# Two layers of a hybrid decoder trunk on one core: attention scores in two visits of one head each, another PSUM pool for the last transposes, and an opening in program order

## The chip, the cores and the metric

The kernel runs on one core of a Trainium2 chip. It computes two whole decoder layers in one launch. The metric is the device time of one execution in microseconds (us), lower is better; a time is the median of several runs. A profiled execution gives a trace with the start and the duration of each instruction on TensorE (PE, with its weight loads as PEld), VectorE (DVE), ScalarE (ACT), GpSimd (POOL) and the DMA queues.

## The reference

Input is `x` (256 tokens of 1024 values), a memory `mem` (256 x 1024), positions, and the weights of both layers, all fp32. Each layer does this:

```python
proj = x @ w_in[l]                                  # 1024 x 7680
q, k, v, cb, cc, cu, qm, gates = jnp.split(proj, IN_SPLITS, axis=-1)
q = rope(q, cos, sin); k = rope(k, cos, sin)        # 8 heads, each with two halves of 64
# differential attention, causal, per head: two softmaxes, one output
sc = einsum('bhcqd,bhckd->bhcqk', qb, kb) * scale   # c = 0, 1
p = softmax(where(causal, sc, -inf)); a = p[:, :, 0] - lam * p[:, :, 1]
o = a @ v; o = o * rsqrt(mean(o * o) + RMS_EPS) * subln_g * (1 - lam_init)
y_conv = short_gated_conv(cb, cc, cu, conv_w[l])    # 3 taps
y_mem = memory_attention(qm, mem, w_mem_kv[l])      # 4 heads over 256 memory tokens
g = sigmoid(gates)
merged = g0 * (y_attn @ w_br_attn) + g1 * (y_conv @ w_br_conv) + g2 * (y_mem @ w_br_mem)
x = layer_norm(ALPHA * x + merged @ w_out, ...)
x = layer_norm(ALPHA * x + grouped_moe(x), ...)     # 16 experts, top 2 of one group of 4
```

## The kernel before, in words

**Stages.** Per layer: keys and values of the memory (`mem_units`, `mv_units`), the transposed input `xT` (`transposed`), the projections with the attention woven between them (`mixers`, `proj`, `attention`, `mem_attention`), the gates, branches and output projection (end of `mixers`), then the router and the experts (`moe`). Weights stream in through SyncE's queue in tiles `raw` of 1 MB, several tiles ahead of their use.

**Split matmuls.** Outside the experts every weight tile is split into a high and a low part, in two halves: ScalarE writes the high part (`hl<-raw`, L180), VectorE the low part (`hl<-raw,hl`, L182). A block of a projection (`ws_block`, L218 to L221) is then 24 matmuls of 256 columns; a unit of `mv_units` (L354) is 12 matmuls of 512. Each such block or unit is one step of a generator and counts as 2600 in the weaving.

**Order of the work.** TensorE's instructions stand in the order in which the program writes them. VectorE's, ScalarE's and GpSimd's are placed by a scheduler, which orders them by its own reckoning; once built, each engine goes through its list strictly in that order.

**The weaving.** In `mixers`, four pairs of attention heads (p = 0 to 3) and two pairs of memory heads (p = 4, 5) are jobs; each job is a generator that is visited with `next(job)`, and `fill(n)` issues blocks of the projections worth n in between. Before the first visit of pair p, blocks are issued until the keys of the pair are in the program; that point comes with the issue of one block of the next projection. A pair of attention heads goes like this: the scores of both heads (`k,q`, L521); on VectorE the causal mask (L526), the maxima (L528) and their scale (L530); on ScalarE the exponentials (L535); on VectorE the reciprocal (L538) and the difference of the two softmaxes (L539 to L543); then TensorE transposes the probabilities (L551), ScalarE copies them (`aT`, L553), TensorE multiplies with the values (L561 to L563), and the result is normalised (`sq` L568, `ss` on GpSimd, `on` L574). The last step, four transposes of `on` (L579) and a split (L209, L210), is made in the middle of the next pair's job.

Before, the visits and fills of a pair are: scores of both heads, fill 5200, last step of the previous pair, fill 5200, transposes of the probabilities, fill 2600, values.

**Keys and queries.** Each projected q or k tile is turned by the rotary tables: four copies on ScalarE (`sw`, L462 and L463), two multiplications and an addition on VectorE (L465 to L467). The tables `sin` and `cos` are made once, in the opening: some 30 small instructions on VectorE (L373 to L392) and two activations on ScalarE (L395, L397).

**PSUM.** `bank()` takes one of four banks of the group "g" (projections, transposes) or one of four of the group "acc" (attention, accumulators). A head's scores take two "acc" banks, the transposed probabilities of a head one, the values of a pair one.

**The opening.** `prow` holds small parameters as rows; TensorE turns them into columns (L408), VectorE derives sums from them (`columns`, L410 to L425), TensorE adds these over partitions (`sums`, L434 and L441), and ScalarE and VectorE read the sums (L435 to L445).

## Time and profile before

| | before |
|---|---|
| median of 3 runs | 1175.45 us (1171.26 to 1175.72) |
| profiled execution, its own time | 1174.08 us |
| its span, first to last instruction | 1172.3 us |
| TensorE busy | 1073.3 us, 92% of the span |
| VectorE busy | 527.9 us, 45% |
| ScalarE busy | 419.4 us, 36% |
| granted TensorE clock, mean | 0.967 of full speed |

How to read it: the span leaves 1.8 us of the profiled execution's time outside. TensorE is busy nearly all the time, so time is lost where it idles or where its clock is granted at half speed (1.2 instead of 2.4 GHz).

### The profile page before, as it was taken

To read this page: it belongs to the slowest core of one execution; us is meant where nothing else is said; L and a number is where in the kernel's file an instruction comes from. 1 tells how busy PE (TensorE), PEld (TensorE's weight loads), DVE (VectorE), ACT (ScalarE), POOL (GpSimd) and SP (SyncE) were. 2 spreads that over 40 slices of the span, in tenths; PEclk is the share of its full clock that TensorE was granted. 3 is DMA by queue.
4 is the path that set the end of the run, shared out by engine and by line. 5 is a ranking of instruction groups with operands and counts; after the bars stand their busy time and mean duration, and the time that the engine had idled before them with its cause. 6 is when DMAs were issued, how large, how long until landed. Compare 5 with 4: busy or idle time off the path is not lost. (4 is left out here: it accounts for less than half of the span.)

```text
span 1172.3 us, 16735 instructions
## 1 busy us (share of the span) xinstructions
PE 1073.3 (92%) x6917; PEld 790.2 (67%) x6917; DVE 527.9 (45%) x874; ACT 419.4 (36%) x730; POOL 42.0 (4%) x87
## 2 busy tenths in 40 slices
PE   4998899999996999999979989999999789999995
PEld 4887899999985334343468868999999543344332
DVE  6667657555544111111367687565546511111114
ACT  3657644444432111010147576454444311011111
POOL 2000000000002000000010000000000110000001
PEclk8999899999998999999989989999999989999998
DMA  9933424556594999999999334345657769999993
GB/s 314 327 121 109 132 84 128 163 185 188 192 369 150 420 421 421 421 422 420 410 303 305 108 101 125 100 144 182 189 194 257 297 262 421 422 421 421 420 420 150
DMA packets 118609, 311.76 MB, mean 266 GB/s; under 512 B 5426, under 2 KB 83440, under 8 KB 93952
## 3 DMA queue, kind: packets, MB, share of 16 engines
q1 hardware_dynamic: 116192, 304.63, 70.2%
q0 software_dynamic: 1760, 5.35, 1.2%
q8 instruction: 56, 0.92, 0.3%
q10 hardware_dynamic: 576, 0.66, 0.2%
q14 instruction: 25, 0.20, 0.0%
HBM read 309.57 MB, written 1.05 MB: 265 GB/s over the span
## 5 line engine op out<-in xcount | busy, mean ns | idle before, releaser
L182 DVE TENSOR_TENSOR hl<-raw,hl 128x1024 fp32r<-128x1024 f32 x192 | 231.2, 1223 | 119.5 <-ACT hl L180 119.2
L218 PE MATMUL ps_g<-th,hl 128*128 128x256 f32 x960 | 244.5, 291 | 20.5 <-ACT hl L180 20.5
L180 ACT ACTIVATE hl<-raw 128x1024 fp32r<-128x1024 f32 x192 | 198.2, 1060 | 127.2 <-PE ps_g L221 60.0
L219 PE MATMUL ps_g<-tl,hl 128*128 128x256 f32 x960 | 240.3, 287 | 0.0
L971 PE MATMUL ps_g<-raw,xg 128*64 128x512 f32 x1024 | 229.4, 598 | 0.0
L218 PEld LDWEIGHTS ps_g<-th,hl 128*128 128x128 f32 x960 | 188.1, 196 | 24.3 <-ACT hl L180 22.0
L219 PEld LDWEIGHTS ps_g<-tl,hl 128*128 128x128 f32 x960 | 188.3, 196 | 0.3
L971 PEld LDWEIGHTS ps_g<-raw,xg 128*64 128x64 f32 x1024 | 71.7, 137 | 134.2 <-issue 131.5
L221 PE MATMUL ps_g<-th,hl 128*128 128x256 f32 x960 | 136.4, 285 | 0.5 <-DVE hl L182 0.5
L221 PEld LDWEIGHTS ps_g<-th,hl 128*128 128x128 f32 x960 | 125.4, 194 | 0.8 <-DVE hl L182 0.8
L1006 PE MATMUL ps_g<-raw,hT 128*64 128x512 f32 x512 | 113.6, 595 | 0.0
L208 DVE TENSOR_TENSOR yl<-ps_g,yh 128x512 fp32r<-128x512 f32 x32 | 22.1, 690 | 150.0 <-ACT yh L207 150.0
L1006 PEld LDWEIGHTS ps_g<-raw,hT 128*64 128x64 f32 x512 | 36.3, 137 | 67.6 <-issue 65.2
L207 ACT ACTIVATE yh<-ps_g 128x512 fp32r<-128x512 f32 x32 | 19.2, 598 | 117.1 <-PE ps_g L1006 117.1
L984 DVE SCALAR_TENSOR_TENSOR h<-ps_g,gs,gate 128x512 f32<-128x512 f32 x16 | 17.8, 1112 | 89.4 <-PE ps_g L971 89.4
L354 PE MATMUL ps_g<-hl,th 128*128 128x512 f32 x192 | 54.4, 417 | 2.0 <-ACT lexp L435 1.5
L995 ACT ACTIVATE hT<-ps_g 128x256 f32<-128x256 f32 x16 | 6.2, 385 | 116.9 <-PE ps_g L993 116.9
L354 PEld LDWEIGHTS ps_g<-hl,th 128*128 128x128 f32 x192 | 37.5, 202 | 12.8 <-issue 2.0
L915 PE MATMUL ps_g<-pf,xh 128*128 128x256 f32 x128 | 30.1, 321 | 13.4 <-DVE pf L898 13.4
L915 PEld LDWEIGHTS ps_g<-pf,xh 128*128 128x128 f32 x128 | 22.9, 218 | 25.5 <-issue 25.1
L920 ACT ACTIVATE xg<-ps_g 128x512 f32<-128x512 f32 x16 | 9.6, 598 | 77.6 <-PE ps_g L915 77.6
L996 DVE COPY hT<-ps_g 128x256 f32<-128x256 f32 x16 | 6.8, 424 | 67.6 <-ACT hT L995 67.6
(235 smaller groups left out, 1302.1 us busy)
## 6 DMA issues: line engine op xcount, KB each, us to landing
raw<-in_w_in SPq DMA_DIRECT2D x64, 1024.0 KB, 5.7
raw<-in_w_exp_gate SPq DMA_DIRECT2D x64, 1024.0 KB, 12.6
raw<-in_w_exp_up SPq DMA_DIRECT2D x64, 1024.0 KB, 14.2
raw<-in_w_exp_down SPq DMA_DIRECT2D x64, 1024.0 KB, 17.0
raw<-in_w_mem_kv SPq DMA_DIRECT2D x8, 1024.0 KB, 12.5
raw<-in_w_br_attn SPq DMA_DIRECT2D x8, 1024.0 KB, 5.1
raw<-in_w_out SPq DMA_DIRECT2D x8, 1024.0 KB, 5.0
raw<-in_w_br_conv SPq DMA_DIRECT2D x8, 512.0 KB, 3.6
```

Source lines behind the costliest of these rows:

```text
L180: nc.scalar.activation(hi, src, AF.Copy)
L182: nc.vector.tensor_tensor(lo, src, hi.bitcast(F32), op=OP.subtract)
L207: return (nc.scalar.activation(hi, src, AF.Copy), nc.vector.tensor_tensor(lo, src, hi.bitcast(F32), op=OP.subtract))
L208: nc.vector.tensor_tensor(lo, src, hi.bitcast(F32), op=OP.subtract))
L218: mm(dst, wh[:, k0 + k, :], ah[:, k, :], start=(k == 0), stop=False)
L219: mm(dst, wh[:, k0 + k, :], al[:, k, :], start=False, stop=False)
L221: mm(dst, wl[:, k0 + k, :], ah[:, k, :], start=False, stop=(k == n - 1))
L354: mm(b[t], a[:, k, t * 128:(t + 1) * 128], ww[:, kk, :], start=(k == 0 and a is ah and ww is wh), stop=(k == KD - 1 and ww is wl))
L915: mm(b[:, a], xs[:, t, (k + a) * 128:(k + a + 1) * 128], pf[:, t], start=(i == 0 and t == 0), stop=(i == 1 and t == 1))
L971: mm(b[both[i]], xg[:, k, c + i * CAP:c + (i + 1) * CAP], w[i][:, kk, :], start=(k == 0), stop=(k == KD - 1))
L984: nc.vector.scalar_tensor_tensor(h.rearrange("q f p -> q p f"), u.rearrange("q (p f) -> q p f", f=4), GS[p // 2][:, p % 2:p % 2 + 1], g.re ...
L1006: mm(bs[c][both[i]], h[:, 2 * j + f, both[i]], w[i][:, f, c * 512:(c + 1) * 512], start=(j == 0 and f == 0), stop=(j == 1 and f == 1))
```

## The change

The scores of a pair are issued in two visits, one head each: `yield` moves into the loop over the heads, in `attention` and in `mem_attention`. The fills of a pair become: fill 2600 (not for the first pair), scores of the first head, fill 2600, last step of the previous pair, scores of the second head, fill 5200, transposes of the probabilities, fill 2600, values. The last transposes of a pair take a bank of the group "g" instead of "acc". And the opening, from the first transposes to the rotary tables, is put under a manual order for VectorE and ScalarE: the instructions written there keep their program order among themselves on these two engines; others may be placed between.

```diff
-APART = (5200, 5200, 2600)
+APART = (2600, 2600, 5200, 2600)
...
+    beginning = tc.manual_schedule(engines={mybir.EngineType.DVE, mybir.EngineType.Activation})
+    beginning.__enter__()
     mT = {0: transposed(mts.pop(0))}
...
         rope[name] = tab
+    beginning.__exit__(None, None, None)
...
             probs[h] = pr[0]
-        yield
+            yield
         aT = []
...
-        b = bank([128, 2, S], "acc")
+        b = bank([128, 2, S])
         for h in range(2):
             for qb in range(2):
                 nc.tensor.transpose(b[:, h, qb * 128:(qb + 1) * 128], on[:, h, qb, :], ident)
...
             probs.append(pr)
-        yield
+            yield
...
+            if prev:
+                fill(APART[0])
             next(job)
-            fill(APART[0])
+            fill(APART[1])
             if prev:
                 next(prev, None)
-            fill(APART[1])
             next(job)
             fill(APART[2])
+            next(job)
+            fill(APART[3])
             next(job)
             prev = job
```

Lines of the changed program from `beginning` on are two or three higher than before (L180, L182 and L207 to L221 stay; L462 is L465, L535 is L538, L553 is L556). The lists of GpSimd and SyncE are the same before and after, but for names and lines. TensorE's list has the same instructions, in the places that the fills say. ScalarE's has three table loads more.

**Place 1, ScalarE's list in the opening.** `sin`, `cos` are the rotary tables, `th` the high part of a transposed input, `hl` that of a weight half, `kv` a copy of finished memory keys (L339) or values (L359). Before:

```order
L397 ACT_TABLE_LOAD
L397 ACTIVATE sin<-r,cc 128x256
L395 ACTIVATE cos<-r 128x256
L207 ACTIVATE th<-ps_g 128x512 x4
L180 ACTIVATE hl<-raw 128x1024 x6
L339 ACTIVATE kv<-ps_g 128x512 x2
L207 ACTIVATE th<-ps_g 128x512 x2
L180 ACTIVATE hl<-raw 128x1024 x2
L207 ACTIVATE th<-ps_g 128x512 x2
```

Now:

```order
L207 ACT_TABLE_LOAD
L207 ACTIVATE th<-ps_g 128x512 x4
L180 ACTIVATE hl<-raw 128x1024 x2
L339 ACTIVATE kv<-ps_g 128x512
L180 ACTIVATE hl<-raw 128x1024 x2
L339 ACTIVATE kv<-ps_g 128x512
L180 ACTIVATE hl<-raw 128x1024 x2
L207 ACTIVATE th<-ps_g 128x512 x4
L180 ACTIVATE hl<-raw 128x1024 x7
```

The two tables went from the head of the list to a place after the first projections (`sin` ahead of the sums, `cos` behind them, each behind a table load of its own), the first six weight halves are cut into three twos with a key copy between them, and the exponentials that follow load their table again.

**Place 2, VectorE's list around the parameter columns** (`pcol` is the first copy of the columns, `wbs` the sums that the matmul L441 needs, `n` and `r` steps of the rotary tables). Before, the columns' instructions stand alone:

```order
L410 COPY pcol<-ps_g 128x62
L182 TENSOR_TENSOR hl<-raw,hl 128x1024
L412 TENSOR_TENSOR lpr<-pcol 128x2
L418 TENSOR_TENSOR wr_470<-wr_raw,pcol 128x128
L419 TENSOR_TENSOR wb<-wr_raw,pcol 128x128
L421 TENSOR_REDUCE wbs<-wr_470 128x16
L421 TENSOR_REDUCE wbs<-wb 128x16
L418 TENSOR_TENSOR wr_476<-wr_raw,pcol 128x128
L419 TENSOR_TENSOR wb<-wr_raw,pcol 128x128
L421 TENSOR_REDUCE wbs<-wr_476 128x16
L421 TENSOR_REDUCE wbs<-wb 128x16
L425 TENSOR_SCALAR subs<-pcol 128x1 x2
```

Now the last twelve of the 27 rows from `pcol` to the last `wbs` read:

```order
L385 SCALAR_TENSOR_TENSOR r<-n,ang 128x256
L422 TENSOR_TENSOR wb<-wr_raw,pcol 128x128
L386 SCALAR_TENSOR_TENSOR r<-n,r 128x256
L424 TENSOR_REDUCE wbs<-wr_473 128x16
L387 SCALAR_TENSOR_TENSOR r<-n,r 128x256
L424 TENSOR_REDUCE wbs<-wb 128x16
L389 TENSOR_SCALAR r<-r 128x256
L422 TENSOR_TENSOR wb<-wr_raw,pcol 128x128
L390 TENSOR_SCALAR n<-r 128x256
L424 TENSOR_REDUCE wbs<-wr_479 128x16
L391 TENSOR_TENSOR r<-r,n 128x256
L424 TENSOR_REDUCE wbs<-wb 128x16
```

The second rotary table is now made between the columns' instructions; fifteen rows of the same mixture stand ahead of these, and among all 27 are thirteen rotary steps, two weight halves and a multiplication with `sin`.

**Place 3, the second pair of heads in layer 0.** ScalarE before, after the eight exponentials of both heads (`yh` is the split of the first pair's last step, `aT` the copies of the transposed probabilities):

```order
L462 ACTIVATE sw<-ps_g 32x512
L463 ACTIVATE sw<-ps_g 32x512
L462 ACTIVATE sw<-ps_g 32x512
L463 ACTIVATE sw<-ps_g 32x512
L209 ACTIVATE yh<-ps_acc,subs 128x512
L180 ACTIVATE hl<-raw 128x1024 x2
L462 ACTIVATE sw<-ps_g 32x512
L463 ACTIVATE sw<-ps_g 32x512
L462 ACTIVATE sw<-ps_g 32x512
L463 ACTIVATE sw<-ps_g 32x512
L180 ACTIVATE hl<-raw 128x1024
L553 ACTIVATE aT<-ps_acc 128x384 x2
```

ScalarE now, after the four exponentials of the first head; the four exponentials here are those of the second head:

```order
L209 ACTIVATE yh<-ps_g,subs 128x512
L180 ACTIVATE hl<-raw 128x1024 x3
L465 ACTIVATE sw<-ps_g 32x512
L466 ACTIVATE sw<-ps_g 32x512
L465 ACTIVATE sw<-ps_g 32x512
L466 ACTIVATE sw<-ps_g 32x512
L180 ACTIVATE hl<-raw 128x1024 x2
L538 ACTIVATE p,sm<-ps_acc,sm 128x128
L538 ACTIVATE p,sm<-ps_acc,sm 128x256
L538 ACTIVATE p,sm<-ps_acc,sm 128x128
L538 ACTIVATE p,sm<-ps_acc,sm 128x256
L556 ACTIVATE aT<-ps_acc 128x384
```

The second head's exponentials went from a place ahead of all copies and weight halves to a place behind the rotary copies of the next pair's keys and five weight halves. VectorE's list at the same pair, from the second head's scaled maxima to its probabilities, before:

```order
L530 TENSOR_SCALAR sm<-sm 128x4
L539 TENSOR_SCALAR sm<-sm,nlam 128x2
L542 TENSOR_SCALAR p<-p,sm 128x128
L542 TENSOR_SCALAR p<-p,sm 128x256
L543 SCALAR_TENSOR_TENSOR p<-p,sm 128x128
L543 SCALAR_TENSOR_TENSOR p<-p,sm 128x256
L538 RECIPROCAL sm<-sm 128x4
L539 TENSOR_SCALAR sm<-sm,nlam 128x2
L542 TENSOR_SCALAR p<-p,sm 128x128
L542 TENSOR_SCALAR p<-p,sm 128x256
L543 SCALAR_TENSOR_TENSOR p<-p,sm 128x128
L543 SCALAR_TENSOR_TENSOR p<-p,sm 128x256
```

and now, from the scaled maxima (one row ahead of these) to the probabilities of the second head:

```order
L469 TENSOR_TENSOR sw<-sw,sin 128x512
L182 TENSOR_TENSOR hl<-raw,hl 128x1024
L468 TENSOR_TENSOR k<-ps_g,cos 128x512
L182 TENSOR_TENSOR hl<-raw,hl 128x1024
L541 RECIPROCAL sm<-sm 128x4
L470 TENSOR_TENSOR k<-k,sw 128x512
L542 TENSOR_SCALAR sm<-sm,nlam 128x2
L182 TENSOR_TENSOR hl<-raw,hl 128x1024
L545 TENSOR_SCALAR p<-p,sm 128x128
L545 TENSOR_SCALAR p<-p,sm 128x256
L546 SCALAR_TENSOR_TENSOR p<-p,sm 128x128
L546 SCALAR_TENSOR_TENSOR p<-p,sm 128x256
```

The rotary steps of the next keys and four weight halves now stand between the second head's maxima and its probabilities.

## Rows read from the trace of the kernel before

**Rows 1.** The page of the profile: the span and the busy time of each engine.

```profile
span 1172.3 us, 16735 instructions
...
PE 1073.3 (92%) x6917; PEld 790.2 (67%) x6917; DVE 527.9 (45%) x874; ACT 419.4 (36%) x730; POOL 42.0 (4%) x87
```

**Rows 2.** TensorE's waits, grouped: waiting group <- engine, tile and line that ended the wait: total us, count, the longest in us.

```profile
PE ps_acc L521 <- DVE k L467: 9.5, 5, 2.8
PE ps_acc L521 <- DVE on L574: 9.0, 2, 4.5
```

**Rows 3.** The timeline of TensorE: start us, duration us, engine, line, operation, tiles, count, and in brackets the idle time before it with what ended it. Scores of the second, third and fourth pair in layer 0, and of the first pair in layer 1.

```profile
95.22 1.58 PE L521 MATMUL ps_acc<-k,q 64*128 64x128 f32 x16 [1.66 <-DVE k L467]
...
119.90 1.64 PE L521 MATMUL ps_acc<-k,q 64*128 64x128 f32 x6 [4.48 <-DVE on L574]
...
148.54 2.42 PE L521 MATMUL ps_acc<-k,q 64*128 64x128 f32 x16 [2.76 <-DVE k L467]
...
642.45 1.36 PE L521 MATMUL ps_acc<-k,q 64*128 64x128 f32 x14 [0.68 <-DVE k L467]
```

**Rows 4.** Stretches after a wait in which the clock was low: start and end, length, busy time and count on each engine, the mean granted clock (PEclk), the DMA share, GB/s. Two stand at scores, the third in the opening, the fourth behind the matmul of the first exponentials.

```profile
119.90:125.22 5.32, 5.32 (x15) 3.90 (x16) 5.21 (x15) 1.73 (x8) 0.00 (x0) 0.50 0.20 71
148.54:152.53 3.99, 3.99 (x23) 3.31 (x24) 3.87 (x12) 0.62 (x3) 0.00 (x0) 0.57 0.38 107
20.11:26.23 6.12, 6.12 (x28) 6.12 (x29) 6.12 (x7) 4.67 (x5) 0.00 (x0) 0.50 1.08 360
62.67:67.19 4.52, 4.52 (x13) 3.56 (x14) 2.98 (x8) 2.93 (x6) 0.00 (x0) 0.62 0.55 182
```

**Rows 5.** Timeline of ScalarE at the second pair of layer 0.

```profile
98.44 0.37 ACT L535 ACTIVATE p<-ps_acc,sm 128x128 f32<-128x128 f32 x1 [5.32 <-DVE sm L530]
...
105.23 2.00 ACT L180 ACTIVATE hl<-raw 128x1024 fp32r<-128x1024 f32 x2
```

**Rows 6.** Timeline of VectorE at the second pair of layer 0.

```profile
96.18 0.76 DVE L526 TENSOR_TENSOR ps_acc<-ps_acc,cmask 128x256 f32<-128x256 f32 x2 [1.01 <-PE ps_acc L521]
...
100.20 0.18 DVE L538 RECIPROCAL sm<-sm 128x4 f32<-128x4 f32 x1 [0.41 <-ACT p L535]
...
101.14 0.74 DVE L543 SCALAR_TENSOR_TENSOR p<-p,sm 128x128 f32<-128x128 f32 x2
```

**Rows 7.** VectorE, grouped by line and form, from 94 to 180 us: line, tiles, shapes, count | busy us, mean ns | idle before.

```profile
L182 DVE TENSOR_TENSOR hl<-raw,hl 128x1024 fp32r<-128x1024 f32 x18 | 21.6, 1221 | 2.2 <-ACT hl L180 2.2
...
L467 DVE TENSOR_TENSOR k<-k,sw 128x512 f32<-128x512 f32 x3 | 2.1, 687 | 0.0
```

**Rows 8.** Timeline of TensorE at the second pair of layer 0.

```profile
98.75 1.12 PE L221 MATMUL ps_g<-th,hl 128*128 128x256 f32 x8
...
101.63 1.12 PE L221 MATMUL ps_g<-th,hl 128*128 128x256 f32 x8
...
106.33 1.19 PE L354 MATMUL ps_g<-hl,th 128*128 128x512 f32 x4 [0.27 <-ACT hl L180]
...
109.43 0.82 PE L551 MATMUL ps_acc<-ident,p 128*128 128x128 f32 x6
```

**Rows 9.** Timeline of TensorE in the opening.

```profile
8.50 3.46 PE L289 MATMUL ps_g<-ident,mt 128*128 128x128 f32 x15 [1.76 <-DMA mt<-in_mem]
20.11 0.58 PE L218 MATMUL ps_g<-th,hl 128*128 128x256 f32 x1 [8.14 <-ACT hl L180]
...
54.28 0.27 PE L408 MATMUL ps_g<-ident,prow 62*128 62x62 f32 x1
...
60.75 0.43 PE L441 MATMUL ps_g<-wbs,ones 128*128 128x64 f32 x2
62.67 1.20 PE L354 MATMUL ps_g<-hl,th 128*128 128x512 f32 x4 [1.48 <-ACT lexp L435]
```

**Rows 10.** Timeline of ScalarE in the opening.

```profile
8.75 1.28 ACT L397 ACT_TABLE_LOAD   x1 [8.75 <-DMA cc<-consts]
14.96 0.51 ACT L397 ACTIVATE sin<-r,cc 128x256 f32<-128x256 f32 x1 [4.93 <-DVE r L392]
...
17.06 2.04 ACT L207 ACTIVATE th<-ps_g 128x512 fp32r<-128x512 f32 x4
18.97 5.81 ACT L180 ACTIVATE hl<-raw 128x1024 fp32r<-128x1024 f32 x6
28.83 0.60 ACT L339 ACTIVATE kv<-ps_g 128x512 f32<-128x512 f32 x1 [4.05 <-PE ps_g L221]
...
60.54 0.59 ACT L462 ACTIVATE sw<-ps_g 32x512 f32<-32x512 f32 x1 [1.72 <-PE ps_g L221]
61.15 1.28 ACT L435 ACT_TABLE_LOAD   x1
62.45 0.24 ACT L435 ACTIVATE lexp<-ps_g 128x2 f32<-128x2 f32 x2
```

**Rows 11.** Timeline of VectorE in the opening.

```profile
6.94 0.29 DVE L373 CAST posf<-posi 128x256 f32<-128x256 int32 x1 [5.20 <-DMA posi<-in_positions]
...
16.41 0.29 DVE L392 TENSOR_SCALAR r<-r 128x256 f32<-128x256 f32 x1
...
54.59 0.22 DVE L410 COPY pcol<-ps_g 128x62 f32<-128x62 f32 x1 [0.35 <-PE ps_g L408]
...
57.61 0.38 DVE L421 TENSOR_REDUCE wbs<-wb 128x16 f32<-128x128 f32 x1
```

## The prediction

> **What bounds the kernel now.** I read the page first: TensorE is busy 1073.3 of 1172.3 us [rows 1], so only two things can pay: a wait of TensorE, or a stretch in which its clock is low. The grouped waits of TensorE come next. At the lines that the change touches they show two groups, both at the scores L521: 9.5 us for keys that are not turned yet and 9.0 us for `on` [rows 2]. The timeline places them [rows 3]: the second pair's scores start 1.66 late and the fourth's 2.76 late behind `k`, the third's 4.48 late behind `on`; both heads' scores take four "acc" banks, and the previous pair's values still hold one until `on` is made. Last the windows: behind the two longer waits the granted clock is at its lower level, 1.2 GHz, for 5.32 us (0.50) and mostly so for 3.99 us (0.57) [rows 4]. A stretch T at mean clock c loses (1 - c) x T: 2.66 and 1.72 us. Behind the wait of 1.66 no such stretch follows. Neither VectorE (45%) nor ScalarE bounds the kernel, but each is in order, and what stands in its list ahead of a head's softmax is late for TensorE.
>
> **What the change removes.** The one step (2600) ahead of the first head covers the two waits for `k`: a block of 24 matmuls takes 101.63 - 98.75 = 2.88 us [rows 8], more than 1.66 and 2.76. For `on`, the first head takes only two banks, and the second head comes two steps later than the scores stood before: 5.8 against 4.48. The first pair has no fill ahead, so its 0.68 in layer 1 stays [rows 3]. Waits: 9.5 + 9.0 - 0.7 = 17.8. Clock: 2 layers x (2.66 + 1.72) = 8.8. Together **26.6 us** less.
>
> **What it adds at the transposes of the probabilities (L551).** Before, four steps of 2600 lay between the last score and these transposes; that is why L551 came without a wait (at 109.43 no idle time is shown) [rows 8]. Now the second head has two. Two blocks are 5.8 us; at the second pair one block and one memory unit, 2.88 and 109.43 - 106.33 = 3.10, so 6.0 [rows 8]. The lone chain of a head, from the first mask at 96.18 to the end of its fused difference at 101.14 + 0.74 = 101.88, takes 5.7 [rows 6]. Cover and chain are equal, so all that stands between in the lists turns into a wait.
>
> At the **second pair** place 3 shows much between. The next keys' `sw` copies now come ahead of the second head's exponentials, and need the first block behind the scores: 2.88, and 0.3 for the hand-over (my choice; VectorE stood 0.41 before it took over from ScalarE at 100.20 [rows 6]). Then four copies of 0.59 [rows 10], 2.4; two weight halves, 2.0 [rows 5]; four exponentials, from 98.44 [rows 5] to the reciprocal behind them at 100.20 [rows 6], 1.7. Then VectorE: reciprocal to fused difference 100.20 to 101.88, 1.7 [rows 6], with the key addition 0.69 and one weight half 1.22 in between [rows 7], 3.6. Sum 2.88 + 0.3 + 2.4 + 2.0 + 1.7 + 3.6 = 12.9; less 6.0 gives a wait of 6.9 us. Bounds: 4.9 if the two weight halves run during the block, 8.1 if VectorE is one more half (1.22) behind.
>
> At the **other three pairs** less stands between. By the changed lists, the first pair has a table load, 1.28 [rows 10], and two low halves, partly within the first head's own time; the third has two low halves, 2 x 1.22 = 2.4 [rows 7], behind the first head's products, 1.7; the fourth has those products and a split of 0.7. I take 2.6 as the mean, with bounds 1 and 4. Waits: 2 x (6.9 + 3 x 2.6) = 29.4.
>
> Nothing here shows how the clock falls behind these waits. The nearest rows are the same engine's waits of 4.48 and 2.76 [rows 3, 4]. I take 2.66 for the second pair and 1.72 for two of the other three: 2 x 2.66 + 4 x 1.72 = 12.2; bounds 5.3 (only the second pair) and 16. Added at L551: **41.6 us**.
>
> **The last transposes' bank.** They move from an "acc" to a "g" bank. Taken at zero: no wait in the rows at these lines is for a "g" bank, and blocks run on both sides to cover a late one; without that cover it would be up to one copy, 0.6 [rows 10], for each of 8, so 0 to 4.8 in all. Memory heads get their two visits under the same fills; their chain has fewer steps, taken at zero too.
>
> **The opening.** Place 1: before, ScalarE made both tables first, and TensorE stood 8.14 us until 20.11 [rows 9]; the table steps ran on VectorE from 6.94 to 16.41 ahead of all else [rows 11]. Now the first transposes' copies lead. They end behind the last transpose, 8.50 + 3.46 = 11.96 [rows 9], plus one copy 0.6; then one weight half, 5.81 / 6 = 1.0 [rows 10]: the first block starts at about 13.7, 6.4 earlier. Taken back: the key copies (0.60 [rows 10]) now stand ahead of the third and fifth weight half, so the next block waits for a finished one plus copy plus half, 0.60 + 1.0 + some 0.3, twice: 3.8. Then place 2. L408 to L441 is 60.75 - 54.28 = 6.5 on TensorE [rows 9]. In that time VectorE had to do 58.0 - 54.59 = 3.4 with one weight half in it [rows 11]; now 27 rows: 2.2 without the half, 13 table steps of 0.3 = 3.9 (rows of 0.29), two halves 2.4, one multiplication 0.7: 9.2, and `pcol` itself starts up to 2 later because table steps stand ahead of it. 0.3 + 9.2 + 2 - 6.5 = 5.0 of wait at the second sums' matmul. The wait of 1.48 for the first exponentials [rows 9] goes inside it. Clock: the 6.12 us at 0.50 and 4.52 us at 0.62 [rows 4] move, not vanish: 0. Sum -6.4 + 3.8 + 5.0 - 1.5 = **about +1** (bounds -4 and +4).
>
> ScalarE's three added table loads are on the path in two places only, both counted: ahead of `sin`, and at the first pair. Each is the load's row, 1.28: a copy ends at 60.54 + 0.59 = 61.13, the load runs from 61.15 to 62.43, and the exponential starts at 62.45 [rows 10], so nothing but the load itself stands there. The Trainium skill ("ScalarE: Activation LUTs", What ACT_TABLE_LOAD costs) says that a switch costs some 1.28 us of load and 1.38 of drain, 2.66 together. By that the three loads would take 8.0 us of ScalarE and not 3.8, and the time would be some 3 to 4 us longer than the one below (an estimate from that page). The load's own duration agrees with its first part; of the drain the three rows leave no room, and I go by the rows.
>
> **Sum.** -26.6 + 41.6 + 1 = +16. On the profiled execution's own 1174.1 that is 1190, on the median, 1.4 above it, 1191.5. I say **1191 us**.
>
> **Rivals.**
> - *The covers hold.* The second head's chain really fits into its two steps, as the 5.7 against 5.8 to 6.0 would allow if the lists' order cost nothing. For it: VectorE and ScalarE are half idle. Against it: place 3. Time 1174.1 - 26.6 + 1 = 1149. It decides when the second pair's L551 waits under 0.5 us. Chance 0.08.
> - *Only the second pair waits.* 1149 + 2 x (6.9 + 2.66) = 1168. For it: the other pairs' lists are nearly clean. Chance 0.12.
> - *The waits at the scores stay.* The change would then not do what it says: VectorE, which now also has the next keys ahead of the second head, delivers `k` later still, by over the 2.9 of the step. With one wait of 1.7 in each layer and its clock (1.72): +7, 1197. Chance 0.05; it lies inside the range.
> - *All pairs wait longer.* The other three pairs at 4 us each with a low clock behind every one: 6 x 1.4 + 2 x 1.72 + 2 = +14, 1205. Chance 0.08.
> - The forecast with its own bounds, 1176 to 1203: 0.67.
>
> **How the numbers follow.** Within 0.5% (5.9 us) is what a measurement of this kernel can hardly tell from no change: 1169.6 to 1181.3. Faster: 0.08 and half of 0.12: 0.14. Same: the other half and the lower end of the forecast's range, 0.06 + 0.06 = 0.12. Slower: the rest, 0.74. The range runs from 1174, which leaves out the first two rivals, to 1205, which takes in most of the last.
>
> **What would show each step.** No idle time before L524 (the scores' new line) at pairs two to four. Waits at L554 behind VectorE's `p`, the longest some 7 us at the second pair of each layer, 1 to 4 at the others, with the clock at 0.5 to 0.6 for 4 to 5 us behind them. The first block near 13.7, two stops near 2 us before 30, and one of some 5 us at L444 behind `wbs`. The prediction is wrong if L554 starts without idle time at the second pair, or if L524 still waits for `k`.

## The result and the profile after

| | before | changed |
|---|---|---|
| median of 6 runs | 1174.1 us (1170.6 to 1175.7) | 1186.6 us (1182.7 to 1191.2) |
| profiled execution's span | 1172.3 us | 1184.7 us |
| TensorE waits at the scores | 18.5 us | 0.7 us |
| TensorE waits at the transposes of the probabilities | none listed | 25.3 us |

The changed kernel is slower: its time is 1.0107 times that of before, with a 95% interval of 1.0085 to 1.0128. The span grew by 12.4 us. The page of the changed kernel answers to [rows 1]:

```profile
span 1184.7 us, 16725 instructions
...
PE 1077.4 (91%) x6917; PEld 787.2 (66%) x6917; DVE 525.6 (44%) x874; ACT 424.0 (36%) x733; POOL 41.0 (3%) x87
```

TensorE's work is the same, its share is a point lower. Its grouped waits answer to [rows 2]. L524 are the scores, L554 the transposes of the probabilities, L444 the second sums, L218 and L354 blocks and units of the projections:

```profile
PE ps_acc L554 <- DVE p L546: 24.4, 7, 6.2
...
PE ps_g L218 <- ACT hl L180: 15.6, 6, 5.8
...
PE ps_g L444 <- DVE wbs L424: 5.3, 1, 5.3
...
PE ps_acc L554 <- ACT aT L556: 0.9, 1, 0.9
PE ps_acc L524 <- DVE k L470: 0.7, 1, 0.7
```

The waits at the scores are gone but for the first pair's 0.7 us in layer 1, which the forecast left in place. In their stead TensorE waits 24.4 + 0.9 = 25.3 us at the transposes, all but the 0.9 for the probabilities that VectorE makes. The timeline of TensorE in the opening and at the second pair answers to [rows 8, 9]:

```profile
13.37 0.39 PE L218 MATMUL ps_g<-th,hl 128*128 128x256 f32 x1 [1.63 <-ACT hl L180]
...
21.01 0.39 PE L218 MATMUL ps_g<-th,hl 128*128 128x256 f32 x1 [1.63 <-ACT hl L180]
...
28.65 1.20 PE L354 MATMUL ps_g<-hl,th 128*128 128x512 f32 x4 [1.63 <-ACT hl L180]
...
60.47 0.66 PE L444 MATMUL ps_g<-wbs,ones 128*128 128x64 f32 x2 [5.28 <-DVE wbs L424]
```

```profile
97.80 0.93 PE L524 MATMUL ps_acc<-k,q 64*128 64x128 f32 x8
...
102.16 0.93 PE L524 MATMUL ps_acc<-k,q 64*128 64x128 f32 x8
...
108.74 0.49 PE L554 MATMUL ps_acc<-ident,p 128*128 128x128 f32 x3
115.42 1.09 PE L554 MATMUL ps_acc<-ident,p 128*128 128x128 f32 x3 [6.18 <-DVE p L546]
```

In the opening the wait ahead of 13.37 is for the first weight half; those ahead of 21.01 and 28.65 are the two stops behind key copies. The second head's scores start at 102.16, 4.4 us behind the first head's. The transposes of the first head start at 108.74 without a wait, those of the second at 115.42 after 6.18 us of idle time. The windows behind the longest waits answer to [rows 4]; the last is the opening:

```profile
115.42:120.66 5.24, 5.24 (x14) 4.06 (x15) 3.82 (x4) 1.45 (x2) 0.00 (x0) 0.50 0.06 18
694.01:697.52 3.51, 3.50 (x10) 2.71 (x11) 2.39 (x3) 1.45 (x2) 0.00 (x0) 0.50 0.59 199
717.74:721.41 3.67, 3.66 (x17) 3.48 (x18) 2.39 (x4) 2.73 (x5) 0.00 (x0) 0.54 0.00 0
747.60:752.13 4.53, 4.53 (x24) 4.33 (x25) 0.25 (x1) 0.49 (x1) 0.00 (x0) 0.62 0.17 56
60.47:66.05 5.58, 5.23 (x13) 3.89 (x14) 5.58 (x14) 3.50 (x5) 0.00 (x0) 0.50 0.27 93
```

In this execution the first block is no longer slowed, while the wait at the second sums has a longer low stretch behind it than [rows 4] had there. At the attention the clock falls behind the second pair's wait in both layers and behind two more in layer 1, and costs 5.24 x 0.50 + 3.51 x 0.50 + 3.67 x 0.46 + 4.53 x 0.38 = 7.8 us. Behind the smaller waits (1.2, 2.4 and 1.9 us in layer 0, 0.9 in layer 1) it stays at full speed.

**What fills the wait.** From the second head's scores to their transposes the changed kernel's window is this one (columns as in [rows 4]: length, then busy us of TensorE, its weight loads, VectorE, ScalarE, GpSimd):

```profile
102.16:115.42 13.26, 7.08 (x49) 5.96 (x48) 12.80 (x29) 12.61 (x26) 0.00 (x0) 0.94 0.53 158
```

VectorE is busy 12.80 and ScalarE 12.61 of 13.26 us. Before, both heads together took 14.21 us from their scores to the transposes, with VectorE and ScalarE busy for 11.65 and 10.55 of it, and TensorE for all but 0.27:

```profile
95.22:109.43 14.21, 13.94 (x105) 12.50 (x106) 11.65 (x32) 10.55 (x27) 0.00 (x0) 1.00 0.26 79
```

VectorE's and ScalarE's timelines show what stands there:

```profile
103.12 0.42 DVE L529 TENSOR_TENSOR ps_acc<-ps_acc,cmask 128x256 f32<-128x256 f32 x1
...
106.25 1.22 DVE L182 TENSOR_TENSOR hl<-raw,hl 128x1024 fp32r<-128x1024 f32 x1
...
107.92 1.22 DVE L182 TENSOR_TENSOR hl<-raw,hl 128x1024 fp32r<-128x1024 f32 x1
109.05 0.17 DVE L533 TENSOR_SCALAR sm<-sm 128x4 f32<-128x4 f32 x1
...
112.62 0.18 DVE L541 RECIPROCAL sm<-sm 128x4 f32<-128x4 f32 x1
...
115.02 0.74 DVE L546 SCALAR_TENSOR_TENSOR p<-p,sm 128x128 f32<-128x128 f32 x2
```

```profile
103.45 2.97 ACT L180 ACTIVATE hl<-raw 128x1024 fp32r<-128x1024 f32 x3
106.43 0.59 ACT L465 ACTIVATE sw<-ps_g 32x512 f32<-32x512 f32 x1
...
108.85 2.00 ACT L180 ACTIVATE hl<-raw 128x1024 fp32r<-128x1024 f32 x2
110.87 0.37 ACT L538 ACTIVATE p<-ps_acc,sm 128x128 f32<-128x128 f32 x1
...
112.02 0.48 ACT L538 ACTIVATE p<-ps_acc,sm 128x256 f32<-128x256 f32 x1
```

VectorE masks the second head at 103.12, but it has the scaled maxima only at 109.05 + 0.17 = 109.2, with the first head's products and two weight halves in between. ScalarE is not free either: three weight halves, four copies, two more halves; its exponentials run from 110.87 to 112.5. The products run from 115.02 to 115.76, and the second head's transposes start at 115.42. Between the maxima and these products VectorE makes three more weight halves (the list of place 3 has three there, not four), so five in all from the mask on. The exponentials start when ScalarE is free, 1.6 us after the maxima: ScalarE's list is the later one here, and VectorE's stands close behind it.

### The profile page after: what moved, and what is told of

The parts are those of the page before. It is cut to its first block, busy times and chain, and to the rows that moved or that the text cites. A ratio compares the mean times of both kernels' runs of the same rounds, so it can differ in the third digit from the quotient of the medians.

```text
span 1184.7 us, 16725 instructions
## 1 busy us (share of the span) xinstructions
PE 1077.4 (91%) x6917; PEld 787.2 (66%) x6917; DVE 525.6 (44%) x874; ACT 424.0 (36%) x733; POOL 41.0 (3%) x87
## 5 line engine op out<-in xcount | busy, mean ns | idle before, releaser
L182 DVE TENSOR_TENSOR hl<-raw,hl 128x1024 fp32r<-128x1024 f32 x192 | 232.4, 1223 | 130.5 <-ACT hl L180 130.2
L218 PE MATMUL ps_g<-th,hl 128*128 128x256 f32 x960 | 245.7, 292 | 15.6 <-ACT hl L180 15.6
L180 ACT ACTIVATE hl<-raw 128x1024 fp32r<-128x1024 f32 x192 | 198.5, 1058 | 140.4 <-PE ps_g L221 62.5
L218 PEld LDWEIGHTS ps_g<-th,hl 128*128 128x128 f32 x960 | 187.8, 196 | 21.0 <-ACT hl L180 17.2
L221 PE MATMUL ps_g<-th,hl 128*128 128x256 f32 x960 | 137.1, 286 | 0.5 <-DVE hl L182 0.5
L221 PEld LDWEIGHTS ps_g<-th,hl 128*128 128x128 f32 x960 | 126.2, 195 | 0.8 <-DVE hl L182 0.8
L207 ACT ACTIVATE yh<-ps_g 128x512 fp32r<-128x512 f32 x32 | 19.1, 597 | 116.9 <-PE ps_g L1012 116.9
L354 PE MATMUL ps_g<-hl,th 128*128 128x512 f32 x192 | 55.8, 420 | 2.0 <-ACT hl L180 1.6
L990 DVE SCALAR_TENSOR_TENSOR h<-ps_g,gs,gate 128x512 f32<-128x512 f32 x16 | 17.8, 1112 | 88.8 <-PE ps_g L977 88.8
L354 PEld LDWEIGHTS ps_g<-hl,th 128*128 128x128 f32 x192 | 37.3, 202 | 11.8 <-issue 2.0
L921 PE MATMUL ps_g<-pf,xh 128*128 128x256 f32 x128 | 29.9, 319 | 13.4 <-DVE pf L904 13.4
## 6 DMA issues: line engine op xcount, KB each, us to landing
raw<-in_w_exp_gate SPq DMA_DIRECT2D x64, 1024.0 KB, 12.6
```

What stands on the lines that cost most here:

```text
L180: nc.scalar.activation(hi, src, AF.Copy)
L182: nc.vector.tensor_tensor(lo, src, hi.bitcast(F32), op=OP.subtract)
L207: return (nc.scalar.activation(hi, src, AF.Copy), nc.vector.tensor_tensor(lo, src, hi.bitcast(F32), op=OP.subtract))
L218: mm(dst, wh[:, k0 + k, :], ah[:, k, :], start=(k == 0), stop=False)
L221: mm(dst, wl[:, k0 + k, :], ah[:, k, :], start=False, stop=(k == n - 1))
L354: mm(b[t], a[:, k, t * 128:(t + 1) * 128], ww[:, kk, :], start=(k == 0 and a is ah and ww is wh), stop=(k == KD - 1 and ww is wl))
```

## The experiments

Each is compared with the kernel before on the same chip. The changed kernel (1.0107) is the other yardstick. Runs 1 to 8 ran on one chip, 9 on a second, 10 and 11 on a third, so times across chips are compared by these ratios.

**1. The opening alone.** The kernel before, with only these lines of the change:

```diff
+    beginning = tc.manual_schedule(engines={mybir.EngineType.DVE, mybir.EngineType.Activation})
+    beginning.__enter__()
...
+    beginning.__exit__(None, None, None)
```

> The kernel before with the opening's manual order alone; the scores and the banks stay as they were. Theory (the opening about pays for itself): the changed kernel's own trace has its first score at 69.36 against 69.95 us, with the first block at 13.4, two stops of 1.6 and one of 5.3 us. So the first score comes 0 to 1 us earlier, the waits at the scores (1.7, 4.5, 2.8 in each layer) stay, and the time is that of the kernel before within 0.4%, 1170 to 1178 us. Rival (the opening carries part of the 12.5 us that the change lost, through what it leaves late for the first layer): 1179 us or more. A third way, it gains by itself: 1169 or less.

Measured: 1177.4 us against 1175.4, ratio 1.0014 (1.0000 to 1.0027). Waits of TensorE:

```profile
PE ps_acc L524 <- DVE k L470: 9.5, 5, 2.8
PE ps_acc L524 <- DVE on L577: 8.9, 2, 4.5
```

The waits at the scores are those of [rows 2], and the wait of 5.3 us at the second sums is there. The opening costs 0 to 3 us, which is the theory. Its first scores are no sooner on the whole: they come at 69.1 to 71.8 us in the traces with the manual order on both engines (changed kernel, runs 1, 5, 7 and 9; in runs 6, 10 and 11 the scheduler placed parts of the opening anew) and at 67.0 to 70.0 in those with the old opening (before, runs 2 to 4).

**2. Without the opening.** The changed kernel without those lines.

> The changed kernel without the manual order of the opening: scores in two visits and the other bank stay. Theory (all of the loss stands at the transposes of the probabilities): their waits stay near 24 us with 6 us at the second pair of each layer, the wait of 5.3 us at the second sums and the two stops of 1.6 go, the start is at 20 us again, and the time is 1183 to 1190 us. Rival (the opening is at fault): 1180 us or less.

Measured: 1184.5 us, ratio 1.0076 (1.0048 to 1.0104).

```profile
PE ps_acc L551 <- DVE p L543: 25.0, 7, 6.2
```

The waits at the transposes are as large as with the opening, 6.2 at the second pair of both layers. They carry the loss; the opening adds at most the 0 to 3 us of run 1.

**3. Two visits alone.** As run 2, and the last transposes take an "acc" bank as before:

```diff
-        b = bank([128, 2, S])
+        b = bank([128, 2, S], "acc")
```

> The kernel before with the scores in two visits and the new fills alone: old opening, and the last transposes in the attention's banks as before. If the bank is worth nothing, as forecast: the same time as without the opening within 0.3%. Rival (the bank is what lets the second head's scores start): waits of 1 to 2 us come back at the scores of the second heads, in pairs three and four; what they add would be taken off the waits at the transposes behind them, so 2 to 4 us either way.

Measured: 1188.0 us, ratio 1.0126 (1.0094 to 1.0158).

```profile
PE ps_acc L551 <- DVE p L543: 20.4, 7, 6.2
...
PE ps_acc L521 <- ACT p L535: 4.7, 4, 1.6
```

The rival is right about the mechanism: with the old bank the second heads' scores of the third and fourth pair wait again, 4.7 us in all, now until the first head's exponentials release their banks, and the transposes wait 20.4 instead of 25.0. Both traces have 0.9 us more for a copy, so the sums are 26.0 and 25.9 us: the waits are alike. The times are not: all four of this run (1187.8 to 1193.0) lie above all four of run 2 (1181.8 to 1186.2), 3.6 us apart by the medians, though the two intervals of the ratios overlap a little. So the move of the bank seems to be worth a few us in the change's favour, by a way that the waits do not show; four times each do not size it, and the forecast's zero is doubtful.

**4. One step ahead of the scores, both heads in one visit.** The kernel before with this:

```diff
-APART = (5200, 5200, 2600)
+APART = (2600, 2600, 5200, 2600)
...
+            if prev:
+                fill(APART[0])
             next(job)
-            fill(APART[0])
+            fill(APART[1])
             if prev:
                 next(prev, None)
-            fill(APART[1])
-            next(job)
             fill(APART[2])
             next(job)
+            fill(APART[3])
+            next(job)
```

> The kernel before with one step of 2600 moved from behind the scores to ahead of them; both heads in one visit, old opening, old bank. Three steps instead of four then lie behind the scores and none of the heads comes late. Theory (a step ahead of the scores removes their waits, and only the second head's lost cover cost time): of the waits of 17.8 us some 2 x 1.6 stay for the wait of 4.5 (a step hides 2.9 of it), the low clock behind the scores (8.8 us) goes but for 1 to 3, the transposes of the probabilities wait 0 to 3 us in all: 15 to 22 us less than before, 1152 to 1160 us. Rival (whatever is taken from behind the scores comes back at the transposes): waits of 3 us or more there in most pairs, and 1168 us or more.

Measured: 1157.5 us against 1175.4, ratio 0.9859 (0.9835 to 0.9882): faster than both.

```profile
PE ps_acc L521 <- DVE on L574: 3.4, 2, 1.7
...
PE ps_acc L551 <- DVE p L543: 1.4, 2, 1.1
PE ps_acc L521 <- DVE k L467: 1.3, 2, 0.7
```

Of 18.5 us at the scores 4.7 are left (1.7 for `on` in each layer, as worked out), and the transposes wait 1.4 us in all behind three steps. So the change's first idea, a step ahead of the scores, pays by itself: 17.9 us, where the forecast put down 26.6 for all the waits at the scores and their clock. That the late second head turned it into a loss is tested by run 7.

**5. ScalarE's key copies behind the second head.** The changed kernel with these lines, where `ex` is the last exponential and `after` places what follows behind it:

```diff
+            if h == 1:
+                state["sw"] = ex
             yield
...
-                for o in (0, 64):
+                with after(state.get("sw")):
+                    for o in (0, 64):
```

> The changed kernel, but ScalarE's four rotary copies of the next keys are placed behind the second head's last exponential, where the change had put them ahead of it; nothing else is forced. Theory A (the sum of the prediction: the copies, 2.4 us, stand in the chain): the wait at the second pair falls from 6.2 to about 3.8 in both layers, with less low clock behind it, and the time by 5 to 9 us, to 1178 to 1182. Theory B (VectorE is the later one: in the changed kernel's trace it has the second head's scaled maxima ready only at 109.2 us, 6 us after the mask, with two weight halves and the first head's products in between, and the exponentials start 1.6 later): at most 1.6 of the wait goes, whatever ScalarE does, and the time stays within 0.4% of the changed kernel's, 1182 to 1191.

Measured: 1187.0 us, ratio 1.0096 (1.0069 to 1.0122).

```profile
PE ps_acc L557 <- DVE p L547: 22.5, 7, 5.8
```

The wait at the second pair falls from 6.2 to 5.75 in layer 0 and to 4.75 in layer 1, the time does not move. Theory A's 3.8 us and its gain did not come, but the run does not take the copies' 2.4 us out of the chain either. In layer 0 the scheduler put a sixth weight half of ScalarE in their place:

```profile
109.85 0.35 ACT L539 ACTIVATE p<-ps_acc,sm 128x128 f32<-128x128 f32 x1
```

The exponentials start 1.0 us earlier than in the changed kernel (109.85 against 110.87), behind that half and 0.7 us after VectorE has the maxima (109.2); then VectorE has two halves between the reciprocal and the products, where it had one and the key addition. What the copies alone cost is not shown. Theory B's bound of 1.6 us holds.

**6. The weight halves behind the second head.** The changed kernel; while the cover's steps are issued, both engines' halves are placed behind the second head's last exponential and last product:

```diff
+            if h == 1:
+                state["dve"], state["act"] = fused, ex
             yield
+        state["dve"] = state["act"] = None
```

> The changed kernel, but the weight halves that are first asked for between the second head's scores and the transposes are placed behind that head's softmax, on ScalarE behind its last exponential and on VectorE behind its last product. Theory A (the order alone makes the wait; the halves can come later at no cost): the waits at L554 go, nothing takes their place, 1155 to 1168 us. Theory B (in the two steps of the cover the two engines have more to do than fits, and the halves feed the very blocks that make the cover): the waits at L554 fall below 6 us in all, but waits of TensorE for weight halves come up by as much or more, and the time is 1180 to 1200 us.

Measured: 1200.4 us, ratio 1.0207 (1.0182 to 1.0233).

```profile
PE ps_g L218 <- ACT hl L180: 43.8, 12, 6.7
...
PE ps_g L354 <- DVE p L545: 10.3, 2, 5.2
```

No wait at the transposes is left among TensorE's waits, but 43.8 - 15.6 = 28.2 us more are spent behind weight halves at the blocks and 10.3 at a unit that waits behind the products. Theory B holds (the time is 0.4 us above its range): the halves that stand ahead of the second head are those that feed the cover. Putting them behind moves the wait, and makes it longer. In this run and in runs 10 and 11 the opening is not that of the changed kernel either (the wait at the second sums is 1.9, 3.3 and 3.3 us, not 5.3), so there the waits at the pairs say more than the times.

**7. A long cover with two visits.** The changed kernel with

```diff
-APART = (2600, 2600, 5200, 2600)
+APART = (2600, 0, 7800, 2600)
```

> The changed kernel with fills of 2600, 0, 7800 and 2600 where it has 2600, 2600, 5200 and 2600: still a visit for each head, but the second follows the first with only the last step of the previous pair between them, and three steps lie between it and the transposes. Theory (the length of the cover behind the second head decides): the waits at L554 fall from 25 us to under 4, a wait of some 1.6 us for the previous pair's result may come back at the third pair's scores, and the time is 1153 to 1168 us. Rival (two visits cost by themselves, through the order that the scheduler makes of them): waits at L554 of over 10 us in all and 1175 us or more.

Measured: 1167.1 us against 1175.3, ratio 0.9920 (0.9893 to 0.9946). No wait at L554 is left above the smallest rows; these are new:

```profile
PE ps_g L218 <- ACT hl L180: 19.2, 8, 5.8
...
PE ps_g L221 <- DVE hl L182: 1.9, 3, 0.9
PE ps_g L582 <- DVE on L577: 1.8, 2, 0.9
```

With three steps behind the second head the loss turns into a gain of 8 us, two visits or not. That is the theory, at the upper end of its range: small new waits for weight halves (3.6 us more at L218, 1.4 more at L221) and for `on` (1.8) take a part of the gain back, so two visits are worth less here than the one of run 4. The clock takes more than these waits: behind the wait of 1.84 us ahead of 102.24, and in the same place in layer 1 (671.80), it is at 1.2 GHz for most of 7 us, which costs some 3.4 us a layer:

```profile
102.24:109.70 7.46, 6.94 (x33) 6.64 (x34) 7.39 (x21) 7.46 (x21) 0.00 (x0) 0.54 0.00 0
```

So the 9.6 us between the medians of runs 7 and 4 go, by the traces, to this clock, these waits and the other opening, and not to waits at the transposes.

**8. The faster kernel with VectorE's opening in order.** Run 4 with the opening's lines for VectorE alone:

```diff
+    beginning = tc.manual_schedule(engines={mybir.EngineType.DVE})
```

> The kernel with one step moved ahead of the scores (1157.5 us), and the opening's manual order on VectorE alone; ScalarE's opening is left to the scheduler, which puts the first transposes' copies and six weight halves in a row, without the key copies between. Theory (the two stops of 1.6 us came from ScalarE's order, the one of 5.3 us at the second sums from VectorE's): the first block near 13, no stop behind it before 30 us, a wait of 5 to 7 us at the second sums, the first scores 2 to 4 us earlier, and 1152 to 1157 us. Rival (the low clock behind the longer wait takes the gain back): within 0.3% of 1157.5.

Measured: 1156.6 us against 1175.3, ratio 0.9843 (0.9827 to 0.9860). By ratios it can't be told from run 4.

```profile
PE ps_g L444 <- DVE wbs L424: 5.4, 1, 5.4
```

```profile
68.03 1.58 PE L524 MATMUL ps_acc<-k,q 64*128 64x128 f32 x16
```

The first block starts at 13.6, the two stops for key copies are gone, the 5.4 us at the second sums stay: the stops belong to ScalarE's order, the wait to VectorE's. The first scores come at 68.0, between run 4's 67.0 and the 69.9 of before with the same opening as run 4. So the same opening differs by 3 us from execution to execution with the stretches of low clock in it, which is more than what this opening gains. The time lies in the theory's range and in the rival's, and no gain over run 4 is shown.

**9. Low halves on GpSimd.** The changed kernel; at the second pair, for halves first asked for in the cover:

```diff
-                nc.vector.tensor_tensor(lo, src, hi.bitcast(F32), op=OP.subtract)
+                (nc.gpsimd if state.get("pool") else nc.vector).tensor_tensor(
+                    lo, src, hi.bitcast(F32), op=OP.subtract)
...
+            state["pool"] = h == 1 and p == 1
             yield
+        state["pool"] = False
```

> The changed kernel, but at the second pair of each layer the low weight halves that are first asked for between the second head's scores and the transposes are made by GpSimd, not by VectorE. In VectorE's list two halves then stand between the second head's mask and its products, not five; ScalarE's list is not touched. Theory B as it stands after the runs before (VectorE and ScalarE are both full in the cover, so relieving one helps until the other ends): the second head's exponentials, which ScalarE ended at 112.5 us, bound it, so 1 to 2 us of the wait of 6.2 goes in each layer, and the time is 1180 to 1186 us if GpSimd's halves arrive in time for their blocks. Rival (VectorE alone was the limit): three halves of 1.22, so 3.6 us less wait at the second pair of each layer. A third way: GpSimd takes longer for a half than VectorE's 1.22 us, and the block behind waits for it; then a new wait behind hl and no gain.

Measured: 1192.5 us, ratio 1.0143 (1.0125 to 1.0162), above the changed kernel's 1.0107 (1.0085 to 1.0128), whose interval it just touches. The two halves on GpSimd, and VectorE's row of the same time:

```profile
107.10 4.90 POOL L182 TENSOR_TENSOR hl<-raw,hl 128x1024 fp32r<-128x1024 f32 x2 [14.07 <-DVE p L546]
```

```profile
107.23 5.04 DVE L547 SCALAR_TENSOR_TENSOR p<-p,sm 128x128 f32<-128x128 f32 x2
```

None of the three ways came: the wait at the second pair stays, 6.3 us, and the first head's transposes there now wait 0.8. GpSimd takes 4.90 us for two halves, and for just that time VectorE's two fused products (the first head's), 0.74 us elsewhere, stretch to 5.04. So this run relieves VectorE of nothing, and does not tell the theories apart. The Trainium skill ("SBUF — State Buffer", SBUF: two separate sides) says that VectorE and GpSimd share a pair of ports by an exclusive lock, and that a VectorE operation with two inputs in SBUF and a GpSimd operation that reads SBUF shut each other out for a whole instruction. This trace agrees: the product has two such inputs and stood still for as long as GpSimd ran.

**10. Low halves left out.** In place of run 9: VectorE's work is taken away and given to nobody. The low halves first asked for in the cover are not made, and the matmuls read the high half in their place.

```diff
+            if state.get("skip"):
+                lo = both[:, 0]
+            else:
...
+            state["skip"] = h == 1
             yield
+        state["skip"] = False
```

> The changed kernel without the low weight halves that are first asked for between the second head's scores and the transposes of its probabilities: the matmuls take the high half in their place, so TensorE's work stays, VectorE's falls by 16 of 192 halves, and what is computed is not the reference. It takes VectorE's load away without giving it to GpSimd. Theory B (both engines are full there, each hides behind the other): at the second pair ScalarE's three weight halves, four copies and one more half still stand ahead of the second head's exponentials; the wait falls from 6.2 to 4.5 to 5.2 us, and the time to 1178 to 1185 us. Rival (VectorE alone was the limit): three halves of 1.22 fewer in its list there, a wait of some 2.6 us and 1177 us or less.

Measured: 1181.8 us against 1175.8, ratio 1.0059 (1.0036 to 1.0083).

```profile
PE ps_acc L559 <- DVE p L549: 20.2, 7, 4.3
```

The second pair's wait falls from 6.2 to 4.3 us in both layers: 1.9 us, less than the 3.7 us that VectorE was spared, a little more than theory B said. ScalarE's list still ends the chain: VectorE has the maxima at 109.2, and the exponentials start behind ScalarE's last copy and half at 110.71. That list is one half shorter than in the changed kernel, so the exponentials come 0.9 us sooner after the second head's scores (102.93 here, 102.16 there); only the rest of the 1.9 us is VectorE's relief by itself.

**11. Both relieved.** As run 10, with the key copies behind the second head as in run 5.

> As the kernel before in this call (the same low halves left out), and also with ScalarE's four rotary copies of the next keys placed behind the second head's last exponential. Theory B (both are full): now that both are relieved, the wait at the second pair falls further, to 3.5 to 4.5 us, which is what six weight halves of 1.0 ahead of the exponentials still cost; the copies alone took 0.4 us (layer 0) and 1.4 us (layer 1) off it. Rival (one engine was the limit): no difference from the run with the halves left out.

Measured: 1180.9 us, ratio 1.0056 (1.0035 to 1.0077).

```profile
PE ps_acc L562 <- DVE p L550: 18.7, 7, 3.8
```

```profile
102.65 5.81 ACT L180 ACTIVATE hl<-raw 128x1024 fp32r<-128x1024 f32 x6
108.66 0.37 ACT L542 ACTIVATE p<-ps_acc,sm 128x128 f32<-128x128 f32 x1 [0.20 <-DVE sm L537]
```

The wait falls to 3.3 us in layer 0 and 3.8 in layer 1. Six weight halves of ScalarE, 5.81 us, are still ahead of the exponentials, which then wait 0.20 us for VectorE's maxima: the two lists end together. The whole time of runs 10 and 11 can't be told apart. Relieving one engine gives 0.4 to 1.9 us of the wait, relieving both 2.9 and 2.4, and each less than the work taken out of the lists. That each engine hides the other is borne out in layer 0 (2.9 is more than 0.4 and 1.9 together) and not in layer 1 (2.4 is less than 1.4 and 1.9), so the shares of the two engines stay open.

## Why the prediction was right

The forecast was 1191 us, the measured time 1186.6, in the range and slower as told. Step by step:

| step | forecast | in the trace |
|---|---|---|
| waits at the scores removed | 17.8 | 18.5 - 0.7 = 17.8 |
| low clock behind them removed | 8.8 | gone; no stretch of low clock starts at L524 |
| second pair's wait at the transposes | 6.9 | 6.2 in both layers |
| mean of the other pairs | 2.6 | 2.1 (1.2, 2.4, 1.9; 0.9, 3.3, 3.3) |
| waits at the transposes, sum | 29.4 | 25.3 |
| low clock behind them | 12.2 | 7.8 |
| bank of the last transposes | 0 | no wait; run 3 without the move is 3.6 us slower than run 2 |
| memory heads' two visits | 0 | no wait listed at their lines |
| first block | 13.7 | 13.4 |
| two stops for key copies | 1.9 each | 1.6 each |
| wait at the second sums | 5.0 | 5.3 |
| opening, sum | +1 | first scores 0.6 us earlier in this pair of traces; alone 0 to +3 (run 1) |

**What held.** As forecast, the wait moved from the scores to the transposes, and grew. Run 4 shows the removed part by itself (-17.9 us, with 4.7 us of the waits at the scores left; the forecast of -26.6 was for all of them). Runs 4 and 7 show the added part: with three steps behind the last scores it all but vanishes (1.4 us and none), whether in one visit or two.

**What was sized too high.** The waits by 4 us, the low clock by 4.4. I put a stretch of low clock behind four of the six smaller waits; it came behind two, both over 3 us. Waits and clock at the attention are then +25.3 + 7.8 - 26.6 = +6.5 us, where the forecast had +15.

**Where the rest of the 12.4 us lies, and where luck comes in.** By stretches of the two traces: up to the first scores -0.6; from there to the router +2.9 in layer 0 (281.3 against 278.4 us) and +6.7 in layer 1 (283.9 against 277.3); between the two +3.5; behind them nothing. So the attention grew by 9.6, some 3 us more than its waits and clock. A part of this is TensorE's switching: the sixteen score matmuls of the second pair took 1.51 us up to the next block before (95.22 to 96.73), and now twice 0.85 (97.80 to 98.65, 102.16 to 103.01), 0.2 us more for the pair; the rest stays unplaced. The 3.5 us between lie where the change does nothing: two stretches at half speed were longer in the profiled execution, near 600 and 630 us, and cost 1.7 us more each. Runs 1 and 4, one with the scores as before and the other with the opening as before, have 296.3 and 296.6 us there, against 294.1 in the trace of before and 297.6 in that of the change: most of the 3.5 us is how those two executions fell out, not the change. So the forecast's terms as measured come to +6.5 - 0.6 = +5.9 us, which would have been 1180; the other 6.5 us, that brought the time within 5 us of 1191, are nothing that the forecast reckoned with. The direction was right by its mechanism, the closeness of the number was in part luck.

**What the sum for the second pair had, and what it lacked.** It ran through ScalarE: block, hand-over, four copies, two halves, exponentials, then VectorE's products. The trace has these steps at nearly these sizes. From the end of the second head's scores (102.16 + 0.93 = 103.09) it takes 3.3 us until the copies start (forecast 3.2), 2.4 for the copies, 2.0 for two halves, 1.75 from the first exponential to the reciprocal (1.7) and 3.1 to the end of the products (3.6). What it lacked is that other work ends as late: ScalarE's three weight halves ahead of the copies run to 106.42, just as far as block and hand-over; and VectorE, with the first head's products, the previous pair's split and two halves ahead of the maxima, has these only 1.6 us before ScalarE is free. So a term taken out of the sum does not come back in full: of the 2.4 us of copies 0.4 and 1.4 in run 5, where another half moved up into their place. In the opening, the load ahead of `sin` is called counted, but the sum has no term for it.

**Rivals.** That the covers hold is out: L554 waits at every pair. That the second pair alone waits is out: the others hold 0.9 to 3.3 us each. That the waits at the scores stay is out.

By the drain of 1.38 us for each table load that the Trainium skill states ("ScalarE: Activation LUTs", What ACT_TABLE_LOAD costs) the forecast would have been 3 to 4 us longer. In the changed kernel the load ahead of `cos` runs from 61.39 to 62.67, the copy ahead of it ends at 61.37 and `cos` starts at 62.68, so no room for a drain is seen here either:

```profile
61.17 0.20 ACT L446 ACTIVATE wsum<-ps_g 128x32 f32<-128x32 f32 x1 [0.15 <-PE ps_g L444]
61.39 1.28 ACT L397 ACT_TABLE_LOAD   x1
62.68 0.42 ACT L397 ACTIVATE cos<-r 128x256 f32<-128x256 f32 x1
```

## What to carry to other kernels

A wait of TensorE is hidden by work ahead of the instruction that waits, but that work is taken from the cover behind it: before moving a step, add up what the other engines must do in the cover that is left, the weight halves of the very steps that make the cover among it. Moving half a producer later shortens its consumer's cover by as much; moving one step ahead of the whole of it (run 4) gave 1.4%, splitting it lost 1.1%. Changing a list's order helps only if the engines have slack there (run 6 lost by it); read the busy time of each engine in the window from producer to consumer first (12.8 and 12.6 of 13.3 us here), and only then the order.

## What the runs showed of the hardware that I had not expected

Two operations of GpSimd with both inputs in SBUF held VectorE for their whole time: 0.74 us of products took 5.04 beside GpSimd's 4.90 (run 9). At 2.45 us a half, GpSimd takes twice VectorE's 1.22.

The low clock does not follow every wait of like size. In the changed kernel the granted clock stayed at 2.4 GHz behind waits of 1.9 and 2.4 us in layer 0, but fell to 1.2 GHz behind one of 2.2 at a block (187.74), and behind 3.3 at the transposes. Even the same wait differs: the 1.48 us ahead of the first exponentials' matmul [rows 9] had a low stretch behind it in the trace of before [rows 4], and none in run 4, which has the same instructions up to there. With the low stretch at the first block, also shorter in run 4, this put the first scores at 69.9 us in one and at 67.0 in the other.
